# Seven block products over all tokens for the gated unit and z columns, with the 31-tap convolution as separate jobs

## The chip, the core and the metric

The kernel runs on one core of a Trainium2 chip. Five engines work side by side, each through a queue of its own in a fixed order: PE (TensorE) multiplies matrices into PSUM, DVE (VectorE) does elementwise work, ACT (ScalarE) does functions, copies and casts, POOL (GpSimd) does some elementwise work and issues DMAs, SP (SyncE) issues most DMAs. They wait for each other by semaphores. The metric is the time of one execution on the chip, in device microseconds (us); less is better.

## What is computed

One layer of a decoder: 1024 tokens of 1024 channels. A projection of the normed input feeds a gated unit with a 31-tap convolution, a state space branch (SSD) whose output is gated by z, and two gates; the branches are mixed and normed, and an FFN with a short convolution follows.

```python
h = layer_norm(x, ln_in_g, ln_in_b)
u_glu, z, xbc, dt_raw, gate_a, gate_b = split_in(h @ w_in)
a, g = split(u_glu, 2);  v = a * sigmoid(g)
v = causal_dwconv(v, dw_w, dw_b)                  # 31 taps over tokens
y_a = silu(layer_norm(v)) @ w_conv_out
xbc = silu(causal_dwconv(xbc, conv_w, conv_b))    # 4 taps
y = ssd_chunked(x, dt, a_head, B, C) + x * d      # 32 heads, chunks of 128 tokens
yg = y * silu(z);  yg = yg * rsqrt(mean(yg**2, over each of 4 groups) + eps)
y_b = (yg * norm_w) @ w_ssm_out
mix = (sigmoid(gate_a) * y_a + sigmoid(gate_b) * y_b) @ w_o
h = layer_norm(alpha * h + mix)
h = layer_norm(alpha * h + conv_ffn(h))
```

All products are exact to about float32: each factor is split into a rounded high part and a low part, and a product is three matmuls (high by high, high by low, low by high).

## The kernel before

Tokens are worked in two halves of 512. Channels lie on the 128 partitions, so a column block ("column") of the input projection is 128 output channels by 512 tokens: 8 steps of 128 input channels by 3 matmuls of 128x512, 24 in all (`project`). Its weights come by `weights`: SP loads 128x1024, ACT casts the high part (L156), DVE subtracts it for the low part (L161). In the first half the low part is also stored to DRAM (`low_scr`), and the second half loads it back instead of computing it.

The run of one half is `mixers`, then `combine`, then (first half) `out_proj`; the second half's output projection is within `ffn_blocks`, and the FFN follows for all tokens. `mixers` goes through 4 groups of SSD heads. For a group it makes two columns for B and C, four for x (each with its 4-tap convolution, `conv4`, on ACT and DVE), four for z (`z_gate`, silu on ACT), and two pairs for the gated unit (`glu`: columns CT_A+i and CT_G+i, a sigmoid, a product on DVE); then `ssd_group` works through 4 chunks of 128 tokens. A chunk is a chain over all engines: ACT makes the decay matrix m, DVE masks it (L648), PE multiplies (L653, L656) and updates the state (L661), DVE adds the skip and gates with z (L671, L681). Its tiles m, ab, ce, xs have one buffer each. `scaled` and `parts` then norm a group's result and split it into yT (L722 is the low part on DVE). The first product with the output weights (`ssm_out_first`, groups 0 and 1) is within `mixers`, the second (`weights(wssm[j, 1])`, tile w_sp, groups 2 and 3) is in `combine`.

The 31-tap convolution (`conv31`) runs on DVE: 30 multiply-adds (L564) over 512 tokens for each of 8 channel blocks and each half, 480 in all, two blocks in turn. It is emitted at a lowered priority, `tc.high_priority(offset=-1500)`, so that the scheduler puts its taps where it sees DVE free. The scheduler fixes each engine's order when the program is built, by priorities and a timeline of its own; on the chip an engine takes its queue strictly in that order.

The FFN's up projection already uses seven block products in place of eight for a pair of columns over all 1024 tokens: `ffn_blocks` builds the sums of token blocks, `up_first` does the two products that need the early tokens alone, `up_weights` builds the sums of weight blocks, and `up_rest` does the other five and combines them.

Of the kernel before, what the change touches and what calls it, by code (L numbers as in the profile page):

```python
# [8 lines left out]
F32 = mybir.dt.float32  # L9
# [7 lines left out]
P = 128  # L17
D = 1024
# [43 lines left out]
def kernel(  # L62
# [32 lines left out]
    def bank(which):  # L95
# [26 lines left out]
    v_halo = statep.tile([P, 8, KC - 1], F32, name="v_halo")  # L122
    G.memset(v_halo, 0.0)
    states = [statep.tile([P, HALF], F32, name=f"state{g}") for g in range(GROUPS)]
# [18 lines left out]
        ct: dram.tile([P, D], F32, name=f"low_scr{ct}")  # L143
        for ct in range(CT_N)
        if not CT_GB <= ct < CT_Z
    }
    y_scr = [dram.tile([8, P, HALF], F32, name=f"y_scr{i}") for i in range(2)]
# [138 lines left out]
    def ln_in_first():  # L286
        hT = big_tile("hT0")
        with pool("lnin0", side="right") as pl:
            xts = []
            gb = pl.tile([P, 2 * KD], F32, name="gb_col")  # L290
# [9 lines left out]
            for pair in range(2):  # L300
                with tc.high_priority(offset=3500 if pair else 6000):
                    pts = [bank(0).rearrange("p (k t) -> p k t", k=2) for _ in range(4)]
                    for i in range(2):
                        t = 2 * pair + i
                        mv, rs = ln_stats(pl, xts[t : t + 1], f"in0_{t}", keep=in_norms[t])
                        xh = pl.tile([P, D], F32, tag="xh", bufs=2, name=f"xh{t}")
# [29 lines left out]
                    f = pl.tile([P, KD, 2 * P], F32, tag="f", bufs=2, name=f"f{pair}")  # L336
                    for low in range(2):
# [27 lines left out]
    def ln_in_second(pl, x3):  # L365
# [7 lines left out]
        for t in range(4):  # L373
            xt = x3 if t == 3 else pl.tile([P, D], F32, tag=f"c{t}", name=f"x1_{t}")
# [155 lines left out]
    def glu(pl, hh, hT, i):  # L530
        pa, pg = bank(1), bank(1)
        wa = col_weights(hh, CT_A + i)
        project(pa, wa, hT)
        wg = col_weights(hh, CT_G + i)
        project(pg, wg, hT)
        v = (statep if i & 2 else pl).tile(
            [P, HALF + KC - 1], F32, tag="v", bufs=2, name=f"v{hh}_{i}"
        )
        s = pl.tile([P, HALF], F32, tag="sig", name=f"sig{hh}_{i}")
        A.activation(out=s, in_=pg, func=AF.Sigmoid)  # L540
        A.copy(v[:, : KC - 1], v_halo[:, i, :])
        V.tensor_mul(v[:, KC - 1 :], pa, s)
        if hh == 0:
            A.copy(v_halo[:, i, :], v[:, HALF:])
        return v

    def conv31(pl, hh, vs):

        accs = {}
        for i, v in vs:  # L550
            wc = PC_CW + i * KC
            c = statep.tile([P, HALF], F32, tag="c", bufs=2, name=f"c{hh}_{i}")
            A.activation(  # L553
                out=c,
                in_=v[:, KC - 1 :],
                func=AF.Identity,
                scale=pc[:, wc + KC - 1 : wc + KC],
                bias=pc[:, PC_CB + i : PC_CB + i + 1],
            )
            accs[i] = c  # L560
        for k in range(KC - 1):
            for i, v in vs:
                wc = PC_CW + i * KC
                V.scalar_tensor_tensor(  # L564
                    out=accs[i],
                    in0=v[:, k : k + HALF],
                    scalar=pc[:, wc + k : wc + k + 1],
                    in1=accs[i],
                    op0=ALU.mult,
                    op1=ALU.add,  # L570
                )
        for i, _ in vs:
            if i < 6:
                SY.dma_start(c_scr[hh][i], accs[i])
        return accs

    def z_gate(pl, hh, hT, g):

        zs = pl.tile([P, 4, HALF], F32, tag="zs", bufs=2, name=f"zs{hh}_{g}")
        for i in range(4):  # L580
            silu = A.activation(
                out=zs[:, i, :], in_=column(hh, hT, CT_Z + 4 * g + i), func=AF.Silu
            )
            if g and i:
                issue_after(silu, exps[-1])
        return zs
# [908 lines left out]
```

## Time and profile before

| what | value |
|---|---|
| runs (2) | 1935.47 and 1935.98 us, median 1935.72 |
| span of the profiled execution | 1934.5 us |
| first half: SSD chunks on PE | 107 to 434 us |
| second half's first columns on PE | from 652 us |
| weight loads, DMA mean | 195 GB/s, 376 MB in all |

The profile is of one execution. Busy time of an engine is the time in which it executes; waiting in its queue is not counted. A row of the timeline has its start in the span, its duration, engine, line, operation and the tiles written and read. The slices below divide the span into 40 equal parts and give the busy share in tenths.

```profile
PE   9999999999999999999999999999999999999998
PEld 8888877788888788888888888888888888887886
DVE  7599999999897639899999546597788888888778
ACT  7576767753353366776765435365555555543544
POOL 1001010112300001111112140010000000122010
```

Slices 2 to 9 are the first half's mixers, slices 15 to 21 the second half's.

### The profile page before, as it was taken

How to read it: one execution, taken by the hardware profiler on the slowest of the kernel's cores; microseconds unless marked ns; L12 is line 12 of the kernel's file. 1: busy time of each engine (PE TensorE's matmuls, PEld its weight loads, DVE VectorE, ACT ScalarE, POOL GpSimd, SP SyncE). 2: the span in 40 equal slices, each digit the busy share in tenths (PEclk: the TensorE clock that was granted, in tenths of full speed). 3: DMA queues.
4: the chain of work that ended last, by engine and by line, in shares of the span. 5: the costliest groups of instructions: out<-in, count | busy, mean ns of one | idle time of the engine just before them, and what ended most of it. 6: DMA issues, size and time to landing. Idle time of an engine off the chain costs nothing.

```text
span 1934.5 us, 25807 instructions
## 1 busy us (share of the span) xinstructions
PE 1921.9 (99%) x9424; PEld 1570.4 (81%) x9424; DVE 1600.7 (83%) x2230; ACT 1092.2 (56%) x1641; POOL 216.7 (11%) x256
## 2 busy tenths in 40 slices
PE   9999999999999999999999999999999999999998
PEld 8888877788888788888888888888888888887886
DVE  7599999999897639899999546597788888888778
ACT  7576767753353366776765435365555555543544
POOL 1001010112300001111112140010000000122010
PEclk9999999999999999999999999999999999999999
DMA  6645555547456665656545644566455555479673
GB/s 231 219 169 200 172 201 185 167 160 267 135 183 228 207 208 176 211 177 211 177 162 166 219 143 135 182 241 225 163 171 185 178 185 185 161 276 355 198 250 115
DMA packets 127216, 376.27 MB, mean 195 GB/s; under 512 B 15184, under 2 KB 15728, under 8 KB 127088
## 3 DMA queue, kind: packets, MB, share of 16 engines
q1 hardware_dynamic: 107424, 318.48, 48.7%
q0 software_dynamic: 13184, 44.59, 6.5%
q10 hardware_dynamic: 6480, 11.55, 1.6%
q8 instruction: 74, 1.21, 0.3%
q14 instruction: 54, 0.44, 0.1%
HBM read 290.00 MB, written 84.56 MB: 194 GB/s over the span
## 4 chain that ended last, share of the span: by engine, by line
PE 86%; DVE 9%; DMA 3%; ACT 1%; issue 1%; SPq 0%; DVEq 0%; POOL 0%; ACTq 0%; POOLq 0%
PE acc L192 20%; PE acc L191 20%; PE acc L190 20%; PE sm L190 6%; PE sm L192 6%; PE sm L191 6%; DVE c L564 3%; DMA dr<-wdown 2%; PE sm L653 1%; PE sm L661 1%; PE sm L656 1%; DVE x L517 1%; PE acc L498 1%; DMA st_wo<-wo 1%; PE sm L614 1%
## 5 line engine op out<-in xcount | busy, mean ns | idle before, releaser
L192 PE MATMUL acc<-hT_h,w_c 128*128 128x512 f32 x1000 | 391.4, 392 | 0.0
L191 PE MATMUL acc<-hT_l,w_c 128*128 128x512 f32 x1000 | 391.1, 391 | 0.0
L190 PE MATMUL acc<-hT_h,w_c 128*128 128x512 f32 x1000 | 391.0, 391 | 0.0
L564 DVE SCALAR_TENSOR_TENSOR c<-v,pc,c 128x512 f32<-128x512 f32 x480 | 371.1, 798 | 7.0 <-ACT c L553 4.5
L190 PEld LDWEIGHTS acc<-hT_h,w_c 128*128 128x128 f32 x1000 | 187.8, 188 | 40.6 <-issue 1.9
L192 PEld LDWEIGHTS acc<-hT_h,w_c 128*128 128x128 f32 x1000 | 187.8, 188 | 40.4 <-issue 1.5
L191 PEld LDWEIGHTS acc<-hT_l,w_c 128*128 128x128 f32 x1000 | 187.8, 188 | 39.5 <-issue 1.1
L156 ACT CAST w_c<-st_c 128x1024 fp32r<-128x1024 f32 x128 | 133.8, 1046 | 111.4 <-PE acc L192 84.3
L632 POOL TENSOR_TENSOR ce<-ce,xbc 128x1024 f32<-128x1024 f32 x28 | 78.3, 2796 | 686.8 <-ACT ce L631 686.8
L1260 ACT CAST w_dn<-dr 128x1024 fp32r<-128x1024 f32 (+1 forms) x72 | 67.2, 942 | 76.7 <-DVE dr L1193 36.0
L190 PE MATMUL sm<-h1s,w_s 128*128 128x512 f32 x264 | 102.8, 389 | 0.5 <-ACT fuv L1103 0.5
L191 PE MATMUL sm<-h1s,w_s 128*128 128x512 f32 x264 | 102.7, 389 | 0.0
L192 PE MATMUL sm<-h1s,w_s 128*128 128x512 f32 x264 | 102.2, 389 | 0.0
L621 ACT ACTIVATE m<-ab,acs 128x128 f32<-128x128 f32 x256 | 78.4, 390 | 39.5 <-PE sm L653 37.8
L161 DVE TENSOR_TENSOR w_c<-st_c,w_c 128x1024 fp32r<-128x1024 f32 x62 | 76.7, 1237 | 17.5 <-ACT w_c L156 17.4
L1261 DVE TENSOR_TENSOR w_dn<-dr,w_dn 128x1024 fp32r<-128x1024 f32 (+1 forms) x72 | 77.6, 1084 | 6.3 <-ACT w_dn L1260 6.2
L517 DVE SCALAR_TENSOR_TENSOR x<-u,pc,x 128x512 f32<-128x512 f32 x96 | 78.0, 826 | 5.7 <-ACT x L515 5.6
L192 PE MATMUL acc<-h1b_h,w_ue 128*128 128x512 f32 x176 | 68.7, 395 | 0.3 <-DVE w_ue L161 0.3
L190 PE MATMUL acc<-h1b_h,w_ue 128*128 128x512 f32 x176 | 68.8, 391 | 0.0
L191 PE MATMUL acc<-h1b_l,w_ue 128*128 128x512 f32 x176 | 68.6, 390 | 0.0
L190 PE MATMUL sm<-h1b_h,w_s 128*128 128x512 f32 x176 | 68.5, 389 | 0.0
L191 PE MATMUL sm<-h1b_l,w_s 128*128 128x512 f32 x176 | 68.5, 389 | 0.0
(369 smaller groups left out, 4544.7 us busy)
## 6 DMA issues: line engine op xcount, KB each, us to landing
st_c<-wcol SPq DMA_DIRECT2D x128, 512.0 KB, 4.4
low_scr<-w_c SPq DMA_DIRECT2D x64, 512.0 KB, 2.9
w_c<-low_scr SPq DMA_DIRECT2D x64, 512.0 KB, 4.4
ab<-acs_scr SPq DMA_DIRECT2D x32, 512.0 KB, 4.2
dr<-wdown SPq DMA_DIRECT2D x55, 256.0 KB, 4.9
st_wo<-wo SPq DMA_DIRECT2D x24, 512.0 KB, 4.3
st_ue<-wup SPq DMA_DIRECT2D x22, 512.0 KB, 3.7
first_scr<-first ACTq DMA_DIRECT2D x44, 256.0 KB, 3.0
```

The source lines that it names most:

```text
L156: casts.append(A.copy(w[:, 0, :], st))
L161: sub.tensor_tensor(out=w[:, 1, :], in0=st, in1=w[:, 0, :].bitcast(F32), op=ALU.subtract)
L190: TE.matmul(ps, wa(0), xa(0), start=start, stop=False, skip_group_check=more)
L191: TE.matmul(ps, wa(0), xa(1), start=False, stop=False, skip_group_check=more)
L192: TE.matmul(ps, wa(1), xa(0), start=False, stop=stop, skip_group_check=more)
L498: mm = TE.matmul(pss[o][:, ts], ws[o][:, i, k * P : (k + 1) * P], hT[:, j, k, ts], start=n == 0 and k == 0, stop=n == 2 and k == KD - 1,)
L517: V.scalar_tensor_tensor(out=o, in0=u[:, k : k + HALF], scalar=pc[:, wc + k : wc + k + 1], in1=o, op0=ALU.mult, op1=ALU.add,)
L564: V.scalar_tensor_tensor(out=accs[i], in0=v[:, k : k + HALF], scalar=pc[:, wc + k : wc + k + 1], in1=accs[i], op0=ALU.mult, op1=ALU.add,)
L621: A.activation(out=m[:, h, :], in_=ab[:, h, :], func=AF.Relu, scale=-1.0, bias=acs[:, c, 8 * g + h : 8 * g + h + 1],)
L632: G.tensor_tensor(out=ce, in0=ce, in1=CT[:, cs].unsqueeze(1).to_broadcast([P, 8, P]), op=ALU.mult)
L1260: A.copy(w[:, 0, cs], src)
L1261: V.tensor_tensor(out=w[:, 1, cs], in0=src, in1=w[:, 0, cs].bitcast(F32), op=ALU.subtract)
```

## The change

The columns of the gated unit and z (32 of 72) leave the mixers. They are computed ahead of them for all 1024 tokens, in 16 pairs, each by seven block products. For this the late tokens' input is loaded, normed and transposed early (`in_blocks`; `ln_in_second` still does it again for the second half's other columns), and the head's first results (B, C and x column 0 of group 0, time steps) are finished first and stored (`first_done`, `kept_first`). The gated unit's v goes to DRAM for all tokens (`v_scr`), z after silu as well (`z_scr`). The 31-tap convolution becomes jobs that load v back: `conv31(0, ...)` for the early tokens is emitted in the new stage, `conv31(1, ...)` for the late tokens one block per group within the first half's mixers, two ahead of the first half's `combine`, two within the second half's mixers; with priorities lowered by 3000 or 1500. All eight results now pass through DRAM. The gate_a columns are spread over the groups.

```diff
+def conv31(hh, js, behind):
+    with tc.high_priority(offset=-behind):
+        for i in js:
+            v = convp.tile([P, HALF + KC - 1], F32, tag="v", bufs=2, name=f"v{hh}_{i}")
+            SY.dma_start(v, v_scr[i][:, hh * HALF : (hh + 1) * HALF + KC - 1])
...
+            for k in range(KC - 1):
+                V.scalar_tensor_tensor(
+                    out=c,
+                    in0=v[:, k : k + HALF],
+                    scalar=pc[:, wc + k : wc + k + 1],
+                    in1=c,
+                    op0=ALU.mult,
+                    op1=ALU.add,
+                )
+            SY.dma_start(c_scr[hh][i], c)
...
 def mixers(hh, hT):
-    pre = first_columns(hh, hT, (CT_B, CT_C, CT_X))
+    if hh:
+        pre = first_columns(hh, hT, (CT_B, CT_C, CT_X))
...
-                zs = z_gate(pl, hh, hT, g)
-                vs = [(i, glu(pl, hh, hT, i)) for i in (2 * g, 2 * g + 1)]
+                zs = pl.tile([P, 4, HALF], F32, tag="zs", bufs=2, name=f"zs{hh}_{g}")
+                SY.dma_start(zs, z_scr[hh][g])
                 if g:
                     scaled()
+                    gate_first(pl, hh, hT, (g - 1,))
...
-                with tc.high_priority(offset=-1500):
-                    accs = conv31(pl, hh, vs)
+                if not hh:
+                    conv31(1, (g,), 3000)
+                elif g < 2:
+                    conv31(1, (6 + g,), 1500)
...
+def pair_rest(bl, ws, s, seeded, second_late, second_early, first_late):
+    w24, w10, w3 = ws
+    ps, pz = bank(0), bank(0)
+    if seeded:
+        A.copy(ps, s)
+    product(ps, lambda i: w24[:, i, :HALF], bl["t2"], not seeded)
...
+    A.copy(s, ps)
+    product(pz, lambda i: w3[:, i], bl["t3"], True)
+    product(ps, lambda i: w10[:, i, :HALF], bl["t1"], False)
+    A.copy(second_late, ps)
+    V.tensor_tensor(out=second_late, in0=pz, in1=second_late, op=ALU.subtract)
+    product(pz, lambda i: w10[:, i, HALF:], bl["t4"], False)
+    V.tensor_tensor(out=second_early, in0=pz, in1=s, op=ALU.subtract)
+    product(ps, lambda i: w24[:, i, HALF:], bl["b22"], False)
+    first_late(ps)
+
+def in_blocks(pl, qp, hT, fs, gb):
+    sums = [qp.tile([P, 2, 4, HALF], F32R, name=f"h0s{i}") for i in (1, 2, 3)]
+    b2 = big_tile("h0b2")
...
+    for pair in range(2):
...
+            V.tensor_tensor(out=b11, in0=b11, in1=b12, op=ALU.subtract)
+            V.scalar_tensor_tensor(
+                out=t2, in0=b11, scalar=-1.0, in1=b22, op0=ALU.mult, op1=ALU.subtract
+            )
+            parts(lambda i: sums[2][:, i, :, ts], t2)
...
+def in_first(qp, bl, j):
+    def done(q, ps):
+        f = qp.tile([P, HALF], F32, tag="first", bufs=2, name=f"in_first{q}_{j}")
+        if not q:
+            A.copy(f, ps)
+            A.dma_start(in_first_scr[j][0], f)
...
+    pair_first(bl, wcol[IN_ROWS[j][0]], f"ie{j}", done)
+
+def in_rest(pl, bl, j):
+    ws = pair_weights(pl, *(wcol[ct] for ct in IN_ROWS[j]), f"i{j}", j % 2 or not j)
+    s = pl.tile([P, HALF], F32, tag="s", bufs=2, name=f"is{j}")
+    SY.dma_start(s, in_first_scr[j][0])
...
+        V.tensor_mul(early, early, early_gate)
+        V.tensor_mul(late, late, late_gate)
+        G.dma_start(v_scr[j], v)
...
-    hT = ln_in_first()
-    yT, accs = mixers(0, hT)
-    mixT, hT = combine(0, hT, yT, accs)
+        hT = ln_in_first(pl, gb, fs)
+        first_done(first_columns(0, hT, (CT_B, CT_C, CT_X)))
...
+        bl = in_blocks(pl, qp, hT, fs, gb)
...
+    IN_LEAD = 10
+    in_firsts_to(IN_LEAD)
+    with pool("in") as pl:
+        for j in range(len(IN_ROWS)):
+            in_firsts_to(IN_LEAD + (j + 1) * (len(IN_ROWS) - IN_LEAD) // (len(IN_ROWS) - 1))
+            in_rest(pl, bl, j)
+            if j % 2 and j < 8:
+                conv31(0, (j - 1, j), 3000)
...
+    yT = mixers(0, hT)
+    conv31(1, (4, 5), 1500)
+    mixT, hT = combine(0, hT, yT)
```

`pair_first` and `pair_weights` are the bodies of the former `up_first` and `up_weights`, which now call them with the FFN's weights; the FFN's instructions stay what they were.

The scheduler's order moves with this. In names, c0_6 is the convolution's accumulator of half 0, channel block 6, so c1_4 belongs to the late tokens; w_..._5991 and the like are weights, x4_0_3 is group 3's x of the first half, yT0_2 the split result of groups 2 and 3.

First, DVE's queue at the end of the first half's mixers, up to the last low part of yT. Before:

```order
L564 SCALAR_TENSOR_TENSOR c0_6_4206<-v0_6_3489,pc_99,c0_6_4206 128x512
L161 TENSOR_TENSOR w_gb0_0_4449<-st_gb0_0_4447,w_gb0_0_4449 128x1024
L707 SCALAR_TENSOR_TENSOR x4_0_3_3137<-x4_0_3_3137,pc_99,rstd0_3_4187 128x512 x4
L564 SCALAR_TENSOR_TENSOR c0_7_4208<-v0_7_3557,pc_99,c0_7_4208 128x512
L564 SCALAR_TENSOR_TENSOR c0_6_4206<-v0_6_3489,pc_99,c0_6_4206 128x512
L722 TENSOR_TENSOR yT0_2_l_4080<-x4_0_3_3137,yT0_2_h_4079 128x1024
L564 SCALAR_TENSOR_TENSOR c0_7_4208<-v0_7_3557,pc_99,c0_7_4208 128x512
L161 TENSOR_TENSOR w_gb0_1_4481<-st_gb0_1_4479,w_gb0_1_4481 128x1024
L564 SCALAR_TENSOR_TENSOR c0_6_4206<-v0_6_3489,pc_99,c0_6_4206 128x512
L722 TENSOR_TENSOR yT0_2_l_4080<-x4_0_3_3137,yT0_2_h_4079 128x1024
```

At the same place after the change:

```order
L549 SCALAR_TENSOR_TENSOR c1_4_5822<-v1_4_5820,pc_99,c1_4_5822 128x512
L549 SCALAR_TENSOR_TENSOR c1_5_5857<-v1_5_5855,pc_99,c1_5_5857 128x512
L549 SCALAR_TENSOR_TENSOR c1_4_5822<-v1_4_5820,pc_99,c1_4_5822 128x512
L678 SCALAR_TENSOR_TENSOR x4_0_3_4876<-x4_0_3_4876,pc_99,rstd0_3_5629 128x512 x4
L549 SCALAR_TENSOR_TENSOR c1_5_5857<-v1_5_5855,pc_99,c1_5_5857 128x512
L549 SCALAR_TENSOR_TENSOR c1_4_5822<-v1_4_5820,pc_99,c1_4_5822 128x512
L693 TENSOR_TENSOR yT0_2_l_5590<-x4_0_3_4876,yT0_2_h_5589 128x1024
L549 SCALAR_TENSOR_TENSOR c1_5_5857<-v1_5_5855,pc_99,c1_5_5857 128x512
L693 TENSOR_TENSOR yT0_2_l_5590<-x4_0_3_4876,yT0_2_h_5589 128x1024
```

The taps between these rows were those of the early tokens' last two blocks; now the early tokens' convolution is done by here, and taps of the late tokens' blocks 4 and 5 stand there: 381 taps are ahead of the last row, 141 of them of the late tokens, where there were 216.

Second, DVE's queue where the gated unit is made. Before, between the first half's first columns:

```order
L161 TENSOR_TENSOR w_c0_0_958<-st_c0_0_956,w_c0_0_958 128x1024
L443 COPY acs_112<-sm16_668 128x128
L446 TENSOR_TENSOR wds_110<-dtv_109,edc_111 128x128
L161 TENSOR_TENSOR w_c0_8_988<-st_c0_8_986,w_c0_8_988 128x1024
L161 TENSOR_TENSOR w_c0_1_1026<-st_c0_1_1024,w_c0_1_1026 128x1024
L161 TENSOR_TENSOR w_c0_9_1056<-st_c0_9_1054,w_c0_9_1056 128x1024
L161 TENSOR_TENSOR w_c0_33_1396<-st_c0_33_1394,w_c0_33_1396 128x1024
L542 TENSOR_TENSOR v0_0_1016<-acc24_954,sig0_0_1017 128x512
```

After, in the middle of the new stage (s3_i10, rai10, rbi10, w_s24_i9, w_s10_i8 are weight sums and their parts for pairs 10, 9 and 8, ioc_8 and vt7 are results of pairs 8 and 7):

```order
L1201 TENSOR_TENSOR vt7_2221<-vt7_2221,iol_7_2219 128x512
L549 SCALAR_TENSOR_TENSOR c0_2_1700<-v0_2_1698,pc_99,c0_2_1700 128x512
L549 SCALAR_TENSOR_TENSOR c0_3_1735<-v0_3_1733,pc_99,c0_3_1735 128x512
L1084 TENSOR_TENSOR vt7_2221<-sm53_2224,is7_2216 128x512
L164 TENSOR_TENSOR w_ie13_2462<-st_ie13_2460,w_ie13_2462 128x1024
L549 SCALAR_TENSOR_TENSOR c0_2_1700<-v0_2_1698,pc_99,c0_2_1700 128x512
L549 SCALAR_TENSOR_TENSOR c0_3_1735<-v0_3_1733,pc_99,c0_3_1735 128x512
L1200 TENSOR_TENSOR vt7_2221<-vt7_2221,ioe_7_2218 128x512
L1058 TENSOR_TENSOR s3_i10_2596<-rai10_2592,rbi10_2593 128x512
L1082 TENSOR_TENSOR ioc_8_2384<-sm55_2388,ioc_8_2384 128x512
```

A column cost DVE one low part of 1024; a pair of columns over all tokens now has sums of weight blocks, their low parts and the combining of products, with the taps between them.

More of the change, by code (lines that the diff above doesn't have):

```diff
@@ L1042, in ffn_blocks, with pair_first @@
         }
-    def up_first(qp, bl, j):
-        w = weights(wup[2 * j], f"ue{j}")
+    def pair_first(bl, src, name, done):
+        w = weights(src, name)
         ps = bank(1)
@@ L1077, with up_first, done @@
+    def up_first(qp, bl, j):
+        def done(q, ps):
+            f = qp.tile([P, HALF], F32, tag="first", bufs=4, name=f"first{q}_{j}")
+            A.copy(f, ps)
+            A.dma_start(first_scr[j][q], f)
+        pair_first(bl, wup[2 * j], f"ue{j}", done)
     stores = []
     def up_rest(upp, bl, j, before):
-        w24, w10, w3 = up_weights(upp, j)
+        ws = pair_weights(upp, wup[2 * j], wup[2 * j + 1], f"{j}", j % 2 or not j)
         ug, uv = (
@@ L1369 @@
             SY.dma_start(h1_scr[t * P : (t + 1) * P, :], rs[t])
-    yT, accs = mixers(1, hT)
-    mixT, _ = combine(1, hT, yT, accs)
+    yT = mixers(1, hT)
+    mixT, _ = combine(1, hT, yT)
     state_stack.close()
```

292 lines of the change are left out of this document (183 added, 109 removed).

## The prediction

> **What bounds the kernel now.** I read the page first, then busy time by stage, then both ends of the wait on which the sum rests. The page names two engines that could be the bound.
>
> ```profile
> span 1934.5 us, 25807 instructions
> ...
> PE 1921.9 (99%) x9424; PEld 1570.4 (81%) x9424; DVE 1600.7 (83%) x2230; ACT 1092.2 (56%) x1641; POOL 216.7 (11%) x256
> ```
>
> A busy PE need not be a PE at its pace, and 83% of DVE is a mean over stages. The next view cuts the first half's mixers and what follows them; after the window's length come busy us and instructions of PE, PEld, DVE, ACT and POOL. The last row is from the up projection of the FFN, which already runs seven block products.
>
> ```profile
> 0.00:100.00 100.00, 98.26 (x560) 83.28 (x561) 64.83 (x113) 63.88 (x110) 9.07 (x15) 1.00 0.64 221
> 100.00:200.00 100.00, 100.00 (x535) 80.62 (x533) 99.96 (x151) 68.60 (x122) 9.40 (x5) 1.00 0.54 187
> 200.00:300.00 100.00, 100.00 (x545) 80.25 (x545) 97.99 (x148) 72.50 (x131) 9.61 (x5) 1.00 0.56 195
> 300.00:400.00 100.00, 100.00 (x531) 80.31 (x530) 99.64 (x150) 71.84 (x117) 9.44 (x5) 1.00 0.49 168
> 400.00:474.00 74.00, 74.00 (x401) 59.33 (x400) 74.00 (x111) 39.24 (x59) 9.20 (x10) 1.00 0.62 216
> 474.00:486.00 12.00, 12.00 (x55) 9.93 (x54) 12.00 (x9) 3.13 (x5) 8.84 (x6) 1.00 0.53 186
> 486.00:560.00 74.00, 74.00 (x325) 60.57 (x324) 59.97 (x74) 38.55 (x52) 16.77 (x14) 1.00 0.46 155
> 560.00:650.00 90.00, 90.00 (x415) 75.02 (x414) 69.31 (x97) 26.51 (x36) 2.13 (x4) 1.00 0.57 196
> ...
> 1500.00:1600.00 100.00, 100.00 (x441) 82.22 (x440) 83.14 (x95) 52.82 (x69) 7.68 (x24) 1.00 0.53 181
> ```
>
> Two things are seen. PE is the bound: 441 matmuls in 100 us are 226.8 ns from start to start, and the clock is granted in full. But from 100 to 474 us DVE has hardly an idle moment (2.4 us in 374): PE runs at its pace there because DVE just keeps up. DVE's only reserve ahead of 474 us is the 35.2 us in which it sat idle in the first 100 us, 37.6 us with the 2.4.
>
> How close it is shows where the second half of yT, the normed SSD output of groups 2 and 3, is split for the products of `combine`.
>
> ```profile
> 469.16 1.21 DVE L722 TENSOR_TENSOR yT_l<-x,yT_h 128x1024 fp32r<-128x1024 f32 x1
> 470.30 0.74 DVE L564 SCALAR_TENSOR_TENSOR c<-v,pc,c 128x512 f32<-128x512 f32 x1
> 470.96 1.21 DVE L161 TENSOR_TENSOR w_gb<-st_gb,w_gb 128x1024 fp32r<-128x1024 f32 x1
> 472.09 0.74 DVE L564 SCALAR_TENSOR_TENSOR c<-v,pc,c 128x512 f32<-128x512 f32 x1
> 472.76 1.21 DVE L722 TENSOR_TENSOR yT_l<-x,yT_h 128x1024 fp32r<-128x1024 f32 x1
> ...
> L190 PE MATMUL acc<-yT_h,w_sp x16: 389/389/389, 483.2 to 498.8; 128*128 128x512 f32 x16
> ```
>
> DVE ends the last split at 474.0. PE starts the first product with it at 483.2, and needs group 3's part 12 matmuls later, at 485.9. I call this need P. DVE was 11.9 us early at P.
>
> **The change, term by term.**
>
> *A, PE.* The 32 columns of the gated unit and z took 24 matmuls in each half, 1536; 16 pairs by seven products of 12 take 1344. That is 192 fewer at 226.8 ns: -43.5 us. The late rows of x are transposed once more, 32 transposes.
>
> ```profile
> 19.75 1.75 PE sm L330 x16
> ```
>
> At 0.109 us each that is +3.5. A is -40.0: if nothing else waits, the span is 1894.5.
>
> *B, DVE ahead of P.* Counted in the order of both kernels, these rows stand ahead of the last split of yT in DVE's queue, beyond what stood there: 165 taps of the convolution; 122 two-tensor rows of 512 (sums and low parts of weights, combining of products); 35 of 1024 (low parts of weights and of the block sums); and statistics and scalings of the late rows of x (8 halves of statistics, 4 scalings, 2 sums of 1024, small ones). Prices are start to start.
>
> ```profile
> 911.39 0.76 DVE c L564
> 912.18 0.76 DVE c L564
> ...
> 923.83 3.31 DVE c L564 x5
> ...
> 1044.97 0.68 DVE L638 TENSOR_TENSOR xs<-sm,dtv 128x512 f32<-128x512 f32 x1
> 1045.57 0.68 DVE L643 TENSOR_TENSOR xsd<-sm,wds 128x512 f32<-128x512 f32 x1
> 1046.16 0.28 DVE L636 TENSOR_TENSOR cbm<-sm,upper 128x128 f32<-128x128 f32 x1
> ...
> 4.46 1.29 DVE L231 BATCH_NORM_STATS2 st_in<-x 128x6 f32<-128x512 f32 x2 [2.42 <-DMA x<-x]
> ...
> 7.30 0.76 DVE L308 TENSOR_SCALAR xh<-x,in_norm 128x1024 f32<-128x1024 f32 x1
> ```
>
> Five taps on two channels in turn take 3.31, 0.662 each; alone on one channel they start 0.79 apart. Most stand in turn here, so 0.663. A row of 512 takes 0.60 (1044.97 to 1045.57), one of 1024 1.14 (469.16 to 470.30). So 165 x 0.663 = 109.4, 122 x 0.60 = 73.2, 35 x 1.14 = 39.9, and for the rest 8 x 0.64 + 4 x 0.76 + 2 x 1.2 + 1 = 11.6: 234 us more on DVE.
>
> [...]
>
> PE has 600 matmuls and 32 transposes more ahead of P: 136.1 + 3.5 = 139.6 us. Without a wait it reaches P at 485.9 + 139.6 = 625.5. DVE, with the idle time it has now, ends the split at 474.0 + 234 = 708: PE waits 82. What DVE can win back of its 37.6 idle us bounds this. It idles some 4 us until x lands, whatever happens, so 33 at most, and the wait is at least 49. Above, 5% more on the added rows (12 us) gives 94. In the new stage, from the first pair's product to the first column behind it, PE's rows make 305 us and DVE's 287 (184 taps are 124 of it), so DVE idles about 18 there; with the start that is some 26 to 31, and I take 7 us won back: B is +75 (49 to 94). Behind the waiting product PE's queue holds the columns of gate_b and everything after; casts and sigmoids of ACT wait for their buffers in turn.
>
> *C, P to the last weight of `out_proj`.* DVE has 88 taps there instead of 24, 42.4 us. It idled 14.0 + 20.7 = 34.7 us from 486 to 650. C is +8, from 0 (some of it falls behind the stretch) to 16; I take +7.
>
> *D, second half.* It has 32 columns fewer per PE queue but the same 16 SSD chunks, so PE brings 12.8 us of work from one chunk to the next.
>
> ```profile
> 1020.19 1.05 PE sm L661 x2
> 1040.93 1.06 PE sm L661 x2
> 1056.91 1.06 PE sm L661 x2
> ```
>
> Chunks now follow after 20.7 and 16.0 us, with PE busy in between. D is 0 if they can follow faster, 15 x (16.0 - 12.8) = 48 if not. DVE has 143 us of rows there for 192 of PE, so I stay near zero: +8.
>
> *At nothing:* ACT gains some 31 us (62 copies, 16 fewer long casts), covered by its 27 to 31 idle us in every 100. ACT issues 32 more DMAs and POOL 32, in a stage where POOL is 9% busy. SP's queue is 12 rows shorter: 64 transfers of kept low parts go, pair loads and reloads come, with the DMA share at 0.5 to 0.6. If that cover went, weights would land late: some us for each pair.
>
> Sum: 1934.5 - 40.0 + 75 + 7 + 8 = 1984.5. The runs' median, 1935.72, is 1.2 above this execution's span: 1986.
>
> **Rivals.**
> - *DVE wins back its idle time.* The wait at P is 49 to 65 and D is zero: 1951 to 1974. For it: nothing in DVE's order forces the old idle time. Against: the new stage's products pace DVE.
> - *The second half is paced by its chunks:* D is 30 to 48, 2010 to 2045. For it: no interval under 15 us is in the trace. Against: all were filled by PE.
> - *PE stays the bound,* the other side: 1895 to 1915, decided where the split ends before 625.5. DVE would have to be 76 us shorter ahead of P; if the 141 taps of the later tokens that stand there (94 us) hold nobody, it is. Against: an engine takes its queue in order.
> - *PE is not the bound.* In the trace a saved matmul is worth its 227 ns wherever matmuls follow each other; if it were worth nothing, A would be +3.5 and the time 2029. [...]
>
> **How the numbers follow.** The forecast (1975 to 2010) has 0.52, DVE winning back 0.20, the chunks 0.18, PE as the bound 0.04, PE not the bound 0.03, anything else 0.03. Faster by over 2%, about what a measurement of this kernel can tell from no change, means below 1897: 0.03, most of the PE-bound case. Within 2%, up to 1974.4, is the second case, the rest of the third, and the edge of the first: 0.23. Slower is 0.74. The range 1948 to 2026 holds the forecast and the second case whole (0.72) and 16 of the 35 us of the chunks' case (0.08).
>
> **What would show it.** Right: a gap of PE ahead of the product with yT's second half, some 60 us or more of PE idle time between the new stage and there, a DVE with next to no idle time in it, and PE at 227 ns in the new stage. B is wrong if PE idles but DVE does too: then the chunks' own chain, not DVE's queue, is late. A is wrong if the new stage takes over 320 us. D shows as PE's idle time in the second half's mixers. The forecast falls if the split is done before PE needs it.

## The result, and the profile after

The changed kernel takes 2059.8 us, median of two runs (2056.5 and 2063.1), beside 1935.7 before: a ratio of 1.0635 with a 95% interval of 1.0588 to 1.0683. Slower was forecast, but 2.6% slower, with a range that ended at 2026. The profiled execution has a span of 2054.8 us. First the page: the span, the busy times, and three rows of the 40 slices.

```profile
span 2054.8 us, 25864 instructions
...
PE 1923.2 (94%) x9264; PEld 1554.1 (76%) x9264; DVE 1720.2 (84%) x2398; ACT 1126.6 (55%) x1704; POOL 232.4 (11%) x303
...
PE   8899999997679969989998999999999999999998
DVE  7659999999999999998677865659788888879778
PEclk9999999998789979999999999999999999999999
```

Before, the PE row was all nines but the last. Now it is at six or seven tenths in slices 10 to 12 and 15 and at eight in slices 1, 2, 18 and 22; the granted clock of PE falls in slices 10 to 12 and 15, and DVE is full from slice 4 to 18. Next the busy time by stage (length, then busy us and instructions of PE, PEld, DVE, ACT, POOL, then the granted clock): the start; the new stage up to the first tap at about 150 us and from there on; the first half's mixers up to the first output weight; up to the first product with yT's second half; up to the first weight of the convolution's output product; up to the end of `out_proj`; the second half's mixers up to their first output weight; the rest of the second half; the FFN.

```profile
0.00:39.20 39.20, 34.26 (x255) 30.24 (x255) 31.14 (x65) 21.85 (x42) 8.62 (x17) 0.96 0.63 228
39.20:150.00 110.80, 94.47 (x423) 74.63 (x420) 67.74 (x95) 59.23 (x90) 0.78 (x3) 0.97 0.47 162
150.00:384.70 234.70, 223.02 (x955) 178.66 (x954) 222.72 (x319) 99.39 (x138) 15.24 (x33) 0.99 0.47 153
384.70:619.30 234.60, 188.06 (x986) 147.00 (x985) 229.35 (x344) 160.23 (x293) 26.49 (x16) 0.89 0.52 180
619.30:724.10 104.80, 104.80 (x598) 82.64 (x598) 103.54 (x161) 71.94 (x114) 10.77 (x6) 1.00 0.51 169
724.10:826.60 102.50, 82.94 (x343) 66.06 (x342) 100.15 (x124) 44.75 (x58) 31.11 (x28) 0.88 0.42 131
826.60:931.60 105.00, 94.39 (x421) 76.86 (x421) 103.58 (x152) 30.63 (x41) 3.21 (x7) 0.95 0.58 195
931.60:1136.60 205.00, 193.50 (x1129) 153.46 (x1130) 154.18 (x264) 160.84 (x285) 28.75 (x15) 0.99 0.59 207
1136.60:1411.20 274.60, 274.21 (x1382) 223.81 (x1381) 177.96 (x236) 151.52 (x219) 44.02 (x33) 1.00 0.53 177
1411.20:2054.80 643.60, 633.52 (x2789) 520.74 (x2787) 529.79 (x650) 326.25 (x428) 63.43 (x146) 1.00 0.60 202
```

A busy PE includes matmuls that run late (in the first half's mixers it is busy 188.06 us for some 170 of work), so I use a stage's loss: its length less PE's own work in it. The work is the rows that the kernel's own order has between the same two marks, at the prices of the prediction (0.227 us for a matmul of 512). Summed over the kernel the work is 1863.5 us, 40.1 less than before, as the prediction's term A has it. The loss was 30.9 us before (1934.5 - 1903.6) and is 191.4 now, 160 more. This is where it lies; the two columns on the right are of experiments below.

| stage | own work | loss, changed kernel | loss without the late tokens' taps | loss without any tap |
|---|---|---|---|---|
| new stage | 305 | 40.6 | 43.3 | 37.3 |
| first half's mixers to the first output weight | 170 | 64.7 | 42.3 | 13.6 |
| to the first product with yT's second half | 102 | 2.8 | 4.6 | 2.9 |
| to the convolution's first output weight | 77 | 25.2 | 0.7 | 0.7 |
| to the end of `out_proj` | 90 | 14.3 | 0.0 | 0.0 |
| second half's mixers to the first output weight | 187 | 17.9 | 16.7 | 16.8 |
| rest of the second half | 271 | 4.0 | 4.3 | 3.7 |
| start, FFN and end | 661 | 21.9 | 23.3 | 24.3 |
| all | 1863.5 | 191.4 | 135.2 | 99.3 |

What PE waited for in the first half's mixers, and from the first product with yT's second half to the end of `out_proj` (us in all, times, the longest):

```profile
PE sm L624 <- DVE m L619: 21.5, 3, 7.9
PE acc L193 <- ACT x L518: 19.4, 2, 12.6
PE sm L588 <- DVE x L642: 3.6, 2, 3.3
...
PE acc L193 <- ACT yT_h L692: 12.0, 1, 12.0
PE acc L193 <- DVE r L905: 7.3, 1, 7.3
PE acc L194 <- DVE yT_l L693: 7.0, 2, 6.0
PE acc L467 <- DVE r L905: 2.4, 1, 2.4
```

Need P, which the prediction made the place of the whole wait, has 12.0 + 7.0 us (yT_h and yT_l). More is lost ahead of it, at the mask of a chunk (L619), and at an activation of ScalarE (L518) that stands behind DVE. The timeline of DVE has the first tap here:

```profile
149.37 2.33 DVE L549 SCALAR_TENSOR_TENSOR c<-v,pc,c 128x512 f32<-128x512 f32 x3 [1.44 <-ACT c L541]
```

Ahead of it DVE was idle 8.1 us in the first 39 and 43.1 in the next 111 (the first two rows of the stages), then 12.0 to 384.7 and 5.2 in the first half's mixers. It ends the last split of yT at 755.5 (the last of the four rows of DVE in the section on the hardware).

### The profile page after: what moved, and what is told of

The parts are those of the page before. It is cut to its first block, busy times and chain, and to the rows that moved or that the text cites. A ratio compares the mean times of both kernels' runs of the same rounds, so it can differ in the third digit from the quotient of the medians.

```text
span 2054.8 us, 25864 instructions
## 1 busy us (share of the span) xinstructions
PE 1923.2 (94%) x9264; PEld 1554.1 (76%) x9264; DVE 1720.2 (84%) x2398; ACT 1126.6 (55%) x1704; POOL 232.4 (11%) x303
## 4 chain that ended last, share of the span: by engine, by line
PE 46%; DVE 8%; DMA 4%; ACT 3%; issue 2%; SPq 0%; DVEq 0%; ACTq 0%; POOLq 0%
PE acc L195 9%; PE acc L194 9%; PE acc L193 9%; PE sm L194 6%; PE sm L193 6%; PE sm L195 6%; DVE c L549 2%; DMA dr<-b_scr 1%; DMA dr<-wdown 1%; ACT m L592 1%; DVE w_dn L1406 1%; DMA st_wo<-wo 1%; PE sm L624 1%; PE sm L627 0%; DMA rstd<-nrm_scr 0%
## 5 line engine op out<-in xcount | busy, mean ns | idle before, releaser
L549 DVE SCALAR_TENSOR_TENSOR c<-v,pc,c 128x512 f32<-128x512 f32 x480 | 364.4, 785 | 8.8 <-ACT c L541 8.0
L193 PE MATMUL acc<-hT_h,w_c 128*128 128x512 f32 x488 | 193.5, 397 | 22.3 <-ACT x L518 20.6
L194 PE MATMUL acc<-hT_l,w_c 128*128 128x512 f32 x488 | 192.6, 395 | 0.0
L195 PE MATMUL acc<-hT_h,w_c 128*128 128x512 f32 x488 | 192.1, 395 | 0.0
L193 PEld LDWEIGHTS acc<-hT_h,w_c 128*128 128x128 f32 x488 | 92.7, 190 | 44.0 <-ACT x L518 21.7
L603 POOL TENSOR_TENSOR ce<-ce,xbc 128x1024 f32<-128x1024 f32 x28 | 70.4, 2513 | 487.5 <-ACT ce L602 463.3
L195 PEld LDWEIGHTS acc<-hT_h,w_c 128*128 128x128 f32 x488 | 92.6, 190 | 19.8 <-DVE w_c L164 0.5
L194 PEld LDWEIGHTS acc<-hT_l,w_c 128*128 128x128 f32 x488 | 92.7, 190 | 19.2 <-issue 0.4
L193 PE MATMUL sm<-h0s,w_s_i 128*128 128x512 f32 x192 | 76.6, 400 | 9.5 <-ACT vt L1081 5.0
L159 ACT CAST w_c<-st_c 128x1024 fp32r<-128x1024 f32 x64 | 66.8, 1045 | 31.9 <-PE acc L195 19.0
L624 PE MATMUL sm<-m,xs 128*64 128x128 f32 x512 | 54.3, 295 | 31.7 <-DVE m L619 31.6
L195 PE MATMUL sm<-h0s,w_s_i 128*128 128x512 f32 x192 | 75.2, 395 | 0.3 <-DVE w_s_i L961 0.3
L194 PE MATMUL sm<-h0s,w_s_i 128*128 128x512 f32 x192 | 75.4, 393 | 0.0
L520 DVE SCALAR_TENSOR_TENSOR x<-u,pc,x 128x512 f32<-128x512 f32 x93 | 68.4, 753 | 6.0 <-ACT x L518 5.6
```

Source lines behind the costliest of these rows:

```text
L159: casts.append(A.copy(w[:, 0, :], st))
L193: TE.matmul(ps, wa(0), xa(0), start=start, stop=False, skip_group_check=more)
L194: TE.matmul(ps, wa(0), xa(1), start=False, stop=False, skip_group_check=more)
L195: TE.matmul(ps, wa(1), xa(0), start=False, stop=stop, skip_group_check=more)
L520: V.scalar_tensor_tensor(out=o, in0=u[:, k : k + HALF], scalar=pc[:, wc + k : wc + k + 1], in1=o, op0=ALU.mult, op1=ALU.add,)
L549: V.scalar_tensor_tensor(out=c, in0=v[:, k : k + HALF], scalar=pc[:, wc + k : wc + k + 1], in1=c, op0=ALU.mult, op1=ALU.add,)
```

## The experiments

Each run had the kernel before beside it, at 1935.8 to 1938.4 us. Losses are by each kernel's own order.

### Taps left out, in part and altogether

```diff
-                for k in range(KC - 1):
+                for k in range(0 if hh else KC - 1):
```

> The multiply-adds of the 31-tap convolution for the late tokens (240 rows on VectorE, 141 of them ahead of the last split of yT) are left out; everything else is the changed kernel. Theory 1, VectorE's queue is what the first half waits for: the changed kernel ends that split at 755.5 us; 95 us of rows less would bring VectorE to about 656, so TensorE gets there at its own pace, about 666, some 88 us earlier than now, the waits in the first half's SSD chunks go (65 us to under 15), the new stage stays at about 345 us, and the time is 1940 to 1965. Theory 2, the chain of single-buffered tiles through an SSD chunk paces the first half's mixers whatever VectorE has besides: the waits there stay over 40 us and the time is 2005 to 2045.

2000.9 us (ratio 1.0333, 1.0313 to 1.0354): between both theories. 56 us are gone (span 1998.7). The waits at P and in `out_proj` are gone altogether, as theory 1 has it, but the first half's mixers still lose 42.3 us. Their row in the view by stage comes first, then the same stretch in two parts:

```profile
390.80:603.00 212.20, 182.91 (x986) 143.99 (x985) 182.28 (x277) 163.64 (x298) 25.41 (x16) 0.93 0.60 212
...
390.80:470.00 79.20, 79.15 (x389) 64.20 (x388) 78.16 (x113) 57.83 (x106) 7.86 (x6) 1.00 0.75 271
470.00:603.00 133.00, 103.75 (x599) 79.79 (x598) 104.12 (x165) 105.81 (x193) 17.55 (x10) 0.88 0.52 176
```

DVE is idle 30 us of 212 while PE loses 42, but not at the same time. The 56 early taps that stand here run from 391 to 503 us. Up to 470 DVE is full and PE is still at its pace; behind that PE waits, and DVE has 29 of its 30 idle us. What the stage's sum hides is a queue that is full first and a chain of chunks that is late afterwards. From the start of the stage, the state update of the fourth chunk on PE comes after 109 us here, and after 83 in the next run, without any tap.

```diff
-                for k in range(KC - 1):
+                for k in range(0):
```

> All 480 multiply-adds of the 31-tap convolution are left out. Theory 1 (VectorE's queue): the new stage, 345 us now, loses the part of its 40 us of waits that lies behind 150 us, where the early tokens' taps fill VectorE, and keeps the some 20 us of the start: 320 to 330; with no waits in the first half's chunks the time is 1905 to 1930. Theory 2 (chunk chain): the first half's mixers keep over 40 us of waits, 1970 or more. Theory 3 (weights and block sums are late in the new stage, whatever VectorE does): the new stage stays at 340 or more.

1959.8 us (1955.0 and 1964.5; ratio 1.0121, 1.0088 to 1.0154): still 1.2% slower than before, and 30 us over theory 1's range. By stage, the new stage and the two halves' mixers:

```profile
42.60:384.80 342.20, 316.97 (x1377) 253.88 (x1374) 174.89 (x229) 164.96 (x237) 16.11 (x37) 0.98 0.52 173
384.80:568.50 183.70, 176.44 (x987) 139.89 (x987) 151.37 (x228) 149.85 (x284) 24.31 (x16) 0.99 0.61 218
...
842.00:1045.90 203.90, 195.48 (x1129) 154.85 (x1129) 142.50 (x250) 166.32 (x288) 28.68 (x15) 0.98 0.58 202
```

In the new stage DVE is busy 175 us of 342 and ACT 165, and the stage is as long as with the taps (345.5). So its loss was never theirs. That is theory 3's number for the stage; its cause, late weights and block sums, is not shown by it. The first half's mixers lose 13.6 us, not over 40, so theory 2 falls. All taps together are worth 92 us of span (2054.8 - 1962.8); 68 us over PE's floor (1962.8 - 1894.5) need no tap. The two executions are 10 us apart and the profiled one is the slower; by the medians it is 100 and 64. The price of the taps includes that of the order which they bring, since all queues are ordered anew without them.

Were the taps' 92 us there before?

```diff
-        for k in range(KC - 1):
+        for k in range(0):
             for i, v in vs:
```

> The kernel before with all 480 multiply-adds of the 31-tap convolution left out. In it, too, taps stand among the rows of the SSD chunks, and VectorE was 99% busy there, but a chunk follows the last after 15 to 23 us, filled with two columns of TensorE's work. Theory 1b, taps cost only where TensorE has less work between two chunks than VectorE has rows: they were hidden before, and the time falls by under 8 us, 1928 to 1937. If taps among a chunk's rows delay TensorE by their place whatever stands between the chunks, the kernel before pays for them too, and the time falls by 15 or more.

1935.5 beside 1938.4 us, ratio 0.999 (0.9979 to 1.0002): without any of its 480 taps the kernel before is as fast as with them. Its first half's chunks and what follows, and its second half's, by stage:

```profile
100.00:474.00 374.00, 374.00 (x2013) 301.94 (x2012) 242.91 (x349) 249.19 (x426) 40.10 (x30) 1.00 0.55 192
...
652.00:1120.00 468.00, 466.24 (x2502) 378.20 (x2495) 221.64 (x361) 299.23 (x479) 53.36 (x35) 1.00 0.58 196
```

DVE has a third to a half of its time free here, and nobody gains by it. The taps were wholly hidden; the change has exposed them.

### The taps' place

```diff
-                if not hh:
-                    conv31(1, (g,), 3000)
-                elif g < 2:
-                    conv31(1, (6 + g,), 1500)
...
+                if hh:
+                    conv31(1, (2 * g, 2 * g + 1), 1500, exps[-1])
...
-    conv31(1, (4, 5), 1500)
```

In `conv31` the last argument makes a block's first activation follow that exponential in ScalarE's order. Without that order a later call changes nothing: with all late blocks called in the second half's mixers, DVE's queue came out with the same 141 late taps ahead of P, since the scheduler fills by its own timeline.

> The late tokens' taps are all there, but held back by an order on ScalarE: two channel blocks begin when the first half's last SSD chunk has its exponentials, and two more with each of the second half's next three groups. Ahead of the last split of yT stand 32 of them instead of 141. Theory 1 (VectorE's queue): the split is done at about 670 to 685 instead of 755.5, and behind it VectorE has some 570 us of rows up to the up projection for 615 of TensorE; so the time is 1950 to 1985. Rival, the second half is then paced by VectorE in its mixers: 2000 to 2030. Theory 2 (chunk chain): 2040 or more, with the waits in the first half's chunks unchanged.

2035.2 us (ratio 1.0515, 1.0497 to 1.0534): P is nearly free (5.5 us lost in place of 25.2), `out_proj` loses nothing, and the first half's mixers lose 32.1. But the second half's mixers, which had 17.9, now lose 43.1, and the 11.2 and 4.3 behind them are new. No forecast covers the time, which lies 5 us over the rival's range, but the rival's mechanism holds: the price moves along with the taps. At the end of the second half's mixers DVE has no idle time and PE has 32 us:

```profile
990.00:1101.70 111.70, 79.58 (x484) 61.90 (x485) 111.70 (x176) 76.29 (x137) 18.55 (x10) 0.89 0.38 132
```

```diff
+                if g == 3 and not hh:
+                    conv31(0, (6, 7), 1500, exps[-1])
...
-            if j % 2 and j < 8:
+            if j % 2 and j < 6:
                 conv31(0, (j - 1, j), 3000)
```

(This with the late tokens' taps left out.)

> As the run without the late tokens' taps (2000.9 us; they are left out here too), and the early tokens' last two channel blocks (60 taps) are held back behind the exponentials of the first half's last chunk; before, 58 early taps stood in VectorE's queue among the first half's chunks, where TensorE lost 42 us though VectorE was idle 30. Theory 1b, taps hurt by their place among the rows of a chunk, whatever VectorE's sum: the loss falls to 13 to 20 us and the time to 1974 to 1985, as VectorE has room behind the chunks. Rival, the 42 us are of the order of other rows and of single waits: the time is 1993 to 2005.

1977.6 us, as theory 1b has it. The first half's mixers lose 13.0 us in place of 42.3, about as much as with no tap at all (13.6):

```profile
387.20:570.20 183.00, 176.72 (x987) 139.56 (x985) 150.98 (x226) 150.24 (x285) 25.72 (x17) 0.99 0.63 225
```

The same 60 taps, some 40 us of DVE, cost 29 us ahead of and among the chunks' rows (where 56 of them ran) and 7 us behind them (4.2 at P and 3.6 behind it, in place of 0.7 and 0). So the place of a tap in the queue decides its price: ahead of rows of a chunk for which PE will wait. That this holds whatever else DVE has to do, as the theory words it, is not shown, since the taps stood where DVE was full. PE's order moved as well: from the fourth chunk to the seventh it has 8, 3 and 8 us of PE's own work from one state update to the next with the early taps in their place, and 15, 13 and 15 with the taps held back. How much of the 29 us is due to that order, no run separates.

### The waits that need no tap

These runs look for what sets the 68 us. Kernels without taps are compared with the 1959.8 us above, whose two executions were 10 us apart.

```diff
-    IN_LEAD = 10
+    IN_LEAD = 6
```

> Only the number of first products ahead of the first full pair goes from 10 to 6. In the changed kernel VectorE is idle 51 us in the first 150 because the first tap, at 149 us, needs the second pair's result. Theory 1: the first tap starts at 115 to 130, VectorE's idle time ahead of the last split of yT falls from 72 by 20 to 30 us, 21 more taps of the late tokens are placed ahead of that split (14 us), and the split and the whole come 5 to 18 us earlier: 2038 to 2052. Theory 3 (the pairs' weights arrive late whatever stands first): the first tap moves by less than 10 us and the time is 2050 to 2070.

2040.0 us (ratio 1.0534, 1.0519 to 1.055), within theory 1's range, and by its way: the first tap runs at 122.7 us. The new stage loses 32.6 us in place of 40.6.

```diff
+    in_firsts_to(2)
+    steps_rest()
     in_firsts_to(IN_LEAD)
```

> The changed kernel with 6 first products ahead (the run lead6, 2040.0 us, new stage 334.8 us), and the cumulative sum of the time steps stands 42 matmuls later in TensorE's queue, behind the second pair's first product. If TensorE's 7.4 us wait for VectorE's 16 small rows of the time steps is a cost of its own, the stage falls to 325 to 329 us. If VectorE's queue sets the end of the first half, most of this is given back in the first half's mixers, and the time is 2034 to 2042; if the losses add, it is 2028 to 2034.

2059.0 us: the stage lost 46.8 us, not less. The waits of PE in it, first with 6 products ahead alone, then with the time steps moved:

```profile
PE sm L432 <- DVE sp L422: 7.4, 1, 7.4
PE acc L193 <- ACT in_first L1165: 3.2, 3, 1.7
```

```profile
PE acc L195 <- ACT in_first L1180: 13.3, 2, 12.1
PE acc L195 <- ACT w_ie L159: 4.1, 2, 3.2
```

The wait for the time steps is gone, and one of 12.1 us for ScalarE's copy of a first product, which frees its PSUM bank, has taken its place. Neither forecast was right.

> Both together: late tokens' taps held back to the first half's last chunk and the second half's mixers (alone 2035.2 us, with a new stage of 347.4 us), 6 first products ahead, and the time steps' sum behind the second pair's first product. With the late taps out of its way VectorE has slack ahead of yT's split, so what the start saves should reach the end: 16 to 22 us, 2013 to 2020. If VectorE's queue is what paces all of it, the gain is under 10: 2026 to 2036.

2038.3 us: no gain over the 2035.2 of the held taps alone, and over both forecasts; its new stage lost 47.2 us.

```diff
-            w10 = split_pair(wsp, r2, f"s10_{name}")
+            w10 = split_pair(pl if own else wsp, r2, f"s10_{name}", tag="w10" if own else "w")
```

(With all taps left out; to make room the convolution's tiles v and c have one buffer each, here and in the next run.)

> As the run without the taps (1959.8 us, new stage 342.3 us for 304.7 of TensorE's own work), so all taps are left out, but in the new stage the second of a pair's three weight sums has a buffer of its own in place of one of the three that all weights share. Theory W, in the new stage weights come late because each pair holds two of three shared buffers for its whole length: the stage falls to 325 to 332 us and the time to 1940 to 1952. Theory Q, TensorE waits there on the pair's own chain (a result must be copied out by ScalarE and subtracted by VectorE before its PSUM bank takes the next product) and on the start: the stage stays at 338 to 345 and the time at 1952 to 1965.

1977.2 us, 17 us slower than without the buffer. The stage is 325.8 us long, as theory W has it, but only because the order now begins the next column earlier, with some of the stage's products behind it: by the kernel's own order the loss is 37.2, as without the buffer (37.3), and the mixers lose 29.2 in place of 13.6. Theory W falls.

```diff
-            ab = pl.tile([P, 8, P], F32, tag="ab", name=f"ab{nm}")
+            ab = pl.tile([P, 8, P], F32, tag="ab", bufs=2, name=f"ab{nm}")
```

(And so for m and ce.)

> As the run without the taps, all taps left out; the SSD chunks' tiles for the broadcast sums, the decay matrix and the scaled C (ab, m, ce) have two buffers in place of one. Theory 2b, with VectorE free these single buffers still keep chunks apart: from the first column behind the new stage to the first output weight 183.6 us becomes 172 to 177 (TensorE's work is 170.2), and the same stretch of the second half, 203.9, becomes 188 to 195; the time is 1932 to 1948. Rival, the chunk's chain of engines is serial through its state whatever the buffers: both stretches change by under 4 us, the time by under 8.

1987.7 us, slower by 28 than with single buffers: the mixers lose 18.8 and 26.9 us in place of 13.6 and 16.8. Theory 2b finds no support: a second buffer gave the chunks nothing. Why it cost something isn't settled: the order of all queues moved with it, and v and c had one buffer.

```diff
-                    gate_first(pl, hh, hT, (g - 1,))
+                    gate_first(pl, hh, hT, (2 * g - 2, 2 * g - 1))
...
-                    gate_first(pl, hh, hT, (3,))
+                    gate_first(pl, hh, hT, (6, 7))
...
-            gate_first(pl, hh, hT, range(4, 8))
```

> As the run without the taps (1959.8 us), all taps left out; the eight gate_a columns of a half, of which four stood behind its last SSD chunk, are spread two to a group between the chunks. TensorE's own work is the same; between two chunks it has 1.4 us more. Theory 2c, chunks cannot follow each other faster than some 12 to 15 us through ScalarE, VectorE and TensorE, and the 13 us (first half) and 17 us (second half) that TensorE loses there without any tap come from having too few columns between them: the losses fall to under 5 and under 8 us, and the time to 1936 to 1948. Rival, these losses are waits for single results of ScalarE and VectorE that any order would have: they change by under 5 us in sum, and the time is 1953 to 1966.

1966.9 us: no gain. The mixers lose 9.8 and 11.8 us in place of 13.6 and 16.8, and the stretches up to the next mark 5.9 and 7.9 in place of 2.9 and 2.5. Theory 2c falls; more columns between the chunks moved the loss.

> A whole version: late tokens' taps held back (2035.2 us alone), 6 first products ahead, and two gate_a columns to a group. By theory 2c the second half's mixers, 43 us of loss in the run with the taps held, win some 10 us and the first half's 5; 6 first products ahead saved 10 to 19: 2008 to 2022. By the rival, with VectorE as the second half's pace, only the start is saved: 2022 to 2032. Slower than the 1936 us of the kernel before either way.

2040.1 us: not even the start's gain arrived. The stage lost 30.4 us in place of 42.5, but the second half's products lost it again (30.7 us up to its convolution's output weight, 11.2 with the held taps alone).

In the next run, also without taps, `in_blocks` fills the late tokens' part with a constant and neither loads nor norms nor transposes them.

> As the run without the taps (1959.8 us, loss of TensorE in the new stage 37 us of which some 16 fall in its first 60 us), all taps left out; the late tokens' input is not loaded, normed, transposed and scaled ahead of the new stage either, a constant stands in its place for the block sums. Theory S, the start is paced by ScalarE and VectorE, which make the late rows and their block sums there beside the time steps: the stage's loss falls by 8 to 16 us, and the time to 1940 to 1950, 3.5 of it TensorE's transposes. Rival, the time steps and the order of the queues set the start: the loss falls by under 5 us, 1951 to 1960.

1965.0 us; the stage's loss is 39.4. The late rows cost PE nothing beyond their transposes: theory S falls.

```diff
-        s = pl.tile([P, HALF], F32, tag="s", bufs=2, name=f"is{j}")
+        s = pl.tile([P, HALF], F32, tag="s", bufs=4, name=f"is{j}")
```

> As the run without the taps, all taps left out; the tile into which a pair's stored first result is loaded back has four buffers in place of two. Theory R, behind the start TensorE waits because ScalarE stands still until that result is back (15.6 us in sum in the run without taps), with its casts and copies queued behind: the loss in the new stage falls by 8 to 14 us and the time to 1946 to 1953. Rival, ScalarE would have waited for something else there: under 4 us, 1955 to 1966.

1965.5 us, a loss of 38.8: theory R falls too.

## Why the prediction was wrong

The direction was right, and so was DVE's queue as the place of the largest part. Of the 70 us by which the span was missed (2054.8, forecast 1984.5), some 41 lie in the new stage, to which the sum gave nothing, 18 in B, 7 in C and 6 in D. By cause, the taps and the order that they bring make 92 of the 160 us of added loss, and 68 need no tap. That B and C together, 82 us, come near the taps' 92 is luck: B was priced from all rows added ahead of P, and taps are 109 of its 234 us.

- **A, PE's own work.** The work fell by 40.1 us, as forecast, but no version turned that into time. "If nothing else waits, the span is 1894.5" was then used as if nothing else waited. This is the step that failed. In the new stage I set PE's 305 us against DVE's 287 and concluded that PE keeps its pace; the stage took 345.5, over the 320 that the prediction itself named as the sign of a wrong A. Sums of an engine bound a stage from below only. With DVE at 175 us the stage was 342 us long. Its loss is spread: 95 of the first 111 us are busy, and behind them some 12 us are idle. The time steps' sum was moved, and the late rows, the shared weight buffer and the buffers of the reloaded results were changed one at a time; none gave a gain. 6 products ahead in place of 10 took 8 us off the stage and 20 off the whole. What sets this loss stays open. What was shown is that it isn't the taps.
- **B, DVE ahead of P.** The mechanism was half right. Its signs came: from the end of the new stage to the first product with the low part of yT's second half (752 us) PE is idle 65 us (46.5 in the mixers, 18.1 in the two waits at P) and DVE 9. 93 us are lost between the new stage and the convolution's output weights (64.7 + 2.8 + 25.2), where I had 75 and a range up to 94. Without any tap 17 of it stay. But it was not one wait at P, where "a DVE with next to no idle time" makes PE stand: only 19 us of waits are there. The taps stand between the rows of every chunk, and PE waits for the chunks; 56 early taps alone cost 29 us so. The idle time was mis-sized as well: "I take 7 us won back", 31 us idle in all, against some 71 measured up to 755.5, since no tap can be placed before the second pair's v has been stored (149 us). The average of the stage hid that its work for DVE comes late. Against the 37.6 idle us of the kernel before this is 33 of the 47 us by which the last split came later than the 708 of the prediction; the other 14 were not traced to rows, though the slow rows at P (last section) are among them.
- **C.** Mis-sized: 14.3 in place of 7, all of it taps; it is 0 without the late ones.
- **D.** 17.9 in the second half's mixers where the kernel before lost 4.0: 14 us in place of 8, and taps have at most 1 us of it. My reason, "DVE has 143 us of rows there for 192 of PE", was again a sum against a sum.
- **Rivals.** That the 141 late taps ahead of P hold nobody fell: without the late taps 56 us are gone. DVE winning back its idle time fell; it has 33 us more of it than before. The chunks as the second half's pace had the right place and under half of the size, and whether the chain of a chunk sets that pace was not shown: neither second buffers nor more columns between the chunks gave a gain. That PE was not the bound in the kernel before has no support: without the taps PE is busy there in all 374 us of the first half's chunks, with DVE a third idle.

The change took from the mixers the columns under which a chunk's chain and the taps were hidden. Before, by the order of its queue, PE had 15 to 23 us of work from one chunk of a group to the next and 27 or more from group to group, and 480 taps cost nothing. Now it has 14 us on average in the first half, and from 3 to 24. The chain itself can follow that fast: in the kernel before without its taps, chunks of a group stand 12 to 17 us apart, and PE waits for none of them over 1.2 us. So I read the loss as cover that is gone, under which a delay of a chunk's rows on DVE or ACT did not reach PE. That is argued from these figures; no run gave the mixers their columns back. The version without the convolution's arithmetic is at 1960 us, above the kernel before; no whole version that was tried came below 2035, so none beats it.

## What to carry to other kernels

A matmul that is removed from an engine at its pace can take its cover away with it (here 40.1 us of work went and 160 of loss came): ask, before you count the saving, which chains and which filler rows ran beneath the removed work, and price those as if they stood alone. Engine sums per stage say what a stage can't be faster than, and say nothing about chains that cross engines once no engine is the bound (without the taps the new stage took 342 us, with 305 of PE's own work and DVE busy for 175); an engine that is idle on the mean of a stage can have been full where it mattered (without the late tokens' taps DVE was idle 30 us of 212 in the first half's mixers, but 1 in the first 79). Filler work on an in-order engine is priced by its place ahead of rows that others wait for (the same 60 taps, with the order of PE that each place brought, cost 29 us ahead of and among the chunks' rows and 7 behind them); and the scheduler here, which fills by its own timeline, put it there at the lowered priorities that were tried, until a dependency forbade it.

## What the runs showed of the hardware

Two things made the wait at P dearer here. PE's timeline there (start, duration) reads:

```profile
744.83 0.80 PE L193 MATMUL acc<-yT_h,w_sp 128*128 128x512 f32 x1 [12.05 <-ACT yT_h L692]
751.65 0.79 PE L194 MATMUL acc<-yT_l,w_sp 128*128 128x512 f32 x1 [6.02 <-DVE yT_l L693]
752.24 0.63 PE L195 MATMUL acc<-yT_h,w_sp 128*128 128x512 f32 x1
752.67 0.63 PE L193 MATMUL acc<-yT_h,w_sp 128*128 128x512 f32 x1
```

Behind the wait of 6.02 us matmuls start 0.43 us apart, about twice 0.227, until 759.6, some 8 us. The granted clock is 0.50 from 752 to 759.6, and 0.88 over the stage. After a wait of 2.44 us (from 221.6 us on) they start 0.43 apart too, up to 227.1, with a granted clock of 0.50. After one of 2.53 us, which ended at 170.4, the clock stayed at 1.00, so these waits show no length from which it falls. In the changed kernel some 50 matmuls of 512 start so, at 0.2 us more each some 10 us of the 160.

At the same place POOL adds the convolution's blocks for their mean, and DVE, beside it, does its taps and the last two splits:

```profile
745.58 11.06 POOL L795 TENSOR_TENSOR stats<-stats,cc 128x512 f32<-128x512 f32 x6
```

```profile
745.96 3.42 DVE L549 SCALAR_TENSOR_TENSOR c<-v,pc,c 128x512 f32<-128x512 f32 x2
749.31 2.28 DVE L693 TENSOR_TENSOR yT_l<-x,yT_h 128x1024 fp32r<-128x1024 f32 x1
751.52 1.76 DVE L549 SCALAR_TENSOR_TENSOR c<-v,pc,c 128x512 f32<-128x512 f32 x1
753.20 2.30 DVE L693 TENSOR_TENSOR yT_l<-x,yT_h 128x1024 fp32r<-128x1024 f32 x1
```

A split took 1.21 us before and takes 2.28 here, a tap 1.7 in place of 0.75: beside these adds DVE ran at about half its pace, a factor of 1.9 for the split, where the upper end of B had reckoned with 5%. In both kernels no tap that runs clear of POOL's two-tensor rows takes over 0.76 us, and in both some beside them take up to 2.9. What slows DVE's rows beside them, no run shows.
